# Longer runs of narrow matmuls, each begun after its copies, in one hybrid decoder layer

## The chip, the core and the metric

The kernel is one program on one core of a Trainium2 chip. Its time is the device time of one execution in microseconds (us). The profile shows one further execution, engine by engine: PE is the matrix engine (PEld its weight loads), DVE the vector engine, ACT the scalar engine, POOL the general engine, and SP the engine that issues most transfers.

## What is computed

One step of one decoder layer for two request groups: a prompt of 1024 tokens and 8 decode requests of 4 new tokens each with 1024 tokens of cache.

```python
h = rms_norm(x, g_pre);  u = h @ w_in              # q, k, v, gates of both head groups
# NSA, 8 heads on 2 k/v heads: three attentions, mixed by gates
o_n = g0 * attend(q, compressed_blocks) + g1 * attend(q, top16_blocks) + g2 * attend(q, window_512)
# FoX, 8 heads: softmax attention with accumulated forget gates in the logits
logit = (q @ k.T) * HEAD_DIM ** -0.5 + (cq[t] - ck[s])
o_f = masked_softmax(logit, k_pos <= q_pos) @ v
x = x + rms_norm(concat(o_n * silu(z_n), o_f * silu(z_f)) @ w_out, g_post)
x = x + (p @ w_pproj) * sigmoid(x @ w_pgate)
```

The decode requests compute the same, with keys and values gathered by page from caches in main memory.

## The kernel before

The work of the prompt runs in stages: input projections and compression, FoX attention over four pairs of heads (`fox(j)`, with projections of the next pair in between), NSA attention over four pairs of heads (`nsa(j, ...)`, eight tiles of 128 queries each), output projection, and the last gated addition. The decode requests' attention is written as a generator, `sample_steps()`: `sam_nsa` for two groups of four requests (`gq`), then `sam_fox` for the same two groups. `nsa` calls `advance(w)` after each piece of its own work, which takes some steps of that generator, so decode attention is spread over the NSA tiles.

Program text is not the order on the engines. The framework keeps a priority for each instruction (its place in the program, unless a block changes it), plays the program through a timeline of its own when it is built, and fixes each engine's order from that. Each engine then runs its list strictly in order, with semaphore waits. `add_manual_dep` adds an edge: a NoSync edge only orders two instructions, a Sync edge also makes the later one wait for the earlier one's end.

What the change touches, by names and lines of the kernel before:

- `evac` (L90 to L95) copies a PSUM tile to SBUF, two of three times on ACT (L93), else on DVE (L95).
- `turn` (L655) transposes blocks of probabilities `S` on PE (L659) into a PSUM tile `ps_pt`, of which there are three during NSA, and `evac` copies them back.
- `pv_pairs` (FoX, L676) and `pv_shared` (NSA, L697 and L703) multiply those by values. Their matmuls have 64 output rows, so they use half of PE's columns, and already stand in one order by `follow`.
- `score4` (L823) makes the scores of four decode requests: four matmuls with 32 output rows each, one to each quarter of PE's columns. The quarter is `32 * bl` for request `bl`.
- In `sam_fox`, keys `kp` are transposed (L1207), copied to tiles `ktf` (one of eight buffers named `kt`), and used by score matmuls (L1213) in two halves of eight per chunk of two pages; there are four chunks per group. Values `vp` are used at L1242, and the new tokens' values at L1246.
- In `sam_nsa`, `pv4` (L1129) multiplies probabilities `pts` by selected-branch values `pg` and window values `pgw`; `ktw` are the window keys, `kt_n` the new tokens' keys.

In the profile 128\*32 means a matmul with 128 contraction rows and 32 output rows; float32 matmuls that are no transposes are listed as two instructions each, so x2 is one matmul.

Of the kernel before, what the change touches and what calls it, by code (L numbers as in the profile page):

```python
# [12 lines left out]
AF = mybir.ActivationFunctionType  # L13
# [31 lines left out]
def tile_hymba_step(ctx: ExitStack, tc: tile.TileContext, I: dict, O: dict):  # L45
    nc = tc.nc
# [21 lines left out]
    def mm_tile(tag="fl"):  # L68
        return pst[1].tile([128, 512], F32, name="ps_" + tag, tag=tag, bufs=pst[2][tag])
# [122 lines left out]
    for g0 in (0, 4):  # L192
# [14 lines left out]
        for k in range(KD):  # L207
            ps = mm_tile(("fl", "sc")[k % 2])
# [446 lines left out]
    def turn(S, b0, nb):  # L655
        ps = mm_tile("pt")
        for x in range(nb):
            for a in range(2):
                nc.tensor.transpose(ps[:, (2 * x + a) * 128:(2 * x + a + 1) * 128],  # L659
                                    S[:, a, (b0 + x) * 128:(b0 + x + 1) * 128], ident)  # L660
        evac(S[:, :, b0 * 128:(b0 + nb) * 128].rearrange("p a (x c) -> p x a c", c=128),
             ps[:, :nb * 256].rearrange("p (x a c) -> p x a c", a=2, c=128))

    def follow(ins):

        for x, y in zip(ins, ins[1:]):
            tc.add_manual_dep(y.ins, x.ins.name, mybir.DependencyInfo(mybir.DependencyClass.NoSync,
                                                                      mybir.DependencyReason.DATA), reason="one stretch")

    def pv_pairs(pv, S, V, nblk, mix):  # L670
        for b0 in range(0, nblk, 2):
            turn(S, b0, min(2, nblk - b0))
        ins = []
        for b in reversed(range(nblk)):
            for a in range(2):
                ins.append(nc.tensor.matmul(pv[64 * a:64 * a + 64, :128], lhsT=V[:, b, 64 * a:64 * a + 64],  # L676
                                            rhs=S[:, a, b * 128:b * 128 + 128], start=b == nblk - 1, stop=b == 0))
        follow(ins)
        evac(mix, pv[:, :128], 0.5)

    def pv_shared(pv, S, s3, V, nblk, g, mix):


        odd = nblk % 2
        ps = mm_tile("pt")
        nc.tensor.transpose(ps[:, :128], s3, ident)
        evac(s3, ps[:, :128])
        if odd:
            turn(S, nblk - 1, 1)
            advance(1)  # L690
        for b0 in range(0, nblk - odd, 2):
            turn(S, b0, 2)
            advance(2)
        ins = []
        for b0 in reversed(range(0, nblk - odd, 2)):
            for x in range(2):
                ins.append(nc.tensor.matmul(pv[64 * x:64 * x + 64, :256], lhsT=V[b0 + x],  # L697
                                            rhs=S[:, :, (b0 + x) * 128:(b0 + x + 1) * 128],
                                            start=b0 == nblk - odd - 2, stop=False))
        for k in range(odd + 1):  # L700
            for x in range(2):
                v, p = (V[nblk - 1], S[:, x, (nblk - 1) * 128:nblk * 128]) if k < odd else (vcz[:, g, x], s3)
                ins.append(nc.tensor.matmul(pv[64 * x:64 * x + 64, 128 * x:128 * x + 128], lhsT=v, rhs=p,  # L703
                                            start=False, stop=k == odd))
        follow(ins)
# [383 lines left out]
    def sam_nsa(gq, cmp):  # L1089
# [4 lines left out]
        pgs, kts = [], []  # L1094
        for b in bs:
            pg2, kt = [], []
            for u in range(2):
# [7 lines left out]
                evac(kt[u], ps)  # L1105
# [6 lines left out]
        for c in range(2):  # L1112
            ps = mm_tile("pt")
            score4(ps, q, [[kt[c]] for kt in kts])
            nc.vector.tensor_tensor(sl[:, c * 512:(c + 1) * 512], ps, sb[:, c * 512:(c + 1) * 512], op=OP.add)
            yield
# [10 lines left out]
        def pv4(lhs, rhs, first, last):  # L1127
            for bl in range(4):
                nc.tensor.matmul(pv[32 * bl:32 * bl + 32], lhsT=lhs(bl), rhs=rhs(bl), start=first, stop=last)  # L1129
# [5 lines left out]
        pgs, kts = [], []  # L1135
        for b in bs:
# [6 lines left out]
            evac(kt, ps)  # L1143
# [5 lines left out]
        score4(ps, q, [[kt] for kt in kts])  # L1149
# [8 lines left out]
        for x in range(4):  # L1158
            pv4(lambda bl: pts[:, x, row4(bl)], lambda bl: pgs[bl][:, x, 128:256], False, False)
            yield  # L1160
        pv4(lambda bl: pts[:32, 4, row4(bl)], lambda bl: sv_n[:, 1], False, True)
# [15 lines left out]
    def sam_fox(gq):  # L1177
# [13 lines left out]
        for c in range(4):  # L1191
# [6 lines left out]
            sc = mm_tile("sv")  # L1198
            for j0 in (0, 2):
                kts = []  # L1200
                for kp in kps:
# [6 lines left out]
                    evac(kt, ps.rearrange("p (j c) -> p j c", c=256))  # L1208
                    yield
                    kts.append(kt)  # L1210
# [22 lines left out]
        for x in range(8):  # L1233
# [7 lines left out]
            for bl in range(4):  # L1241
                nc.tensor.matmul(pv[32 * bl:32 * bl + 32], lhsT=pts[:, x, 32 * bl:32 * bl + 32], rhs=vps[bl][:, x % 2],  # L1242
                                 start=x == 0, stop=False)
            yield
        for bl in range(4):
            nc.tensor.matmul(pv[32 * bl:32 * bl + 32], lhsT=pts[:32, 8, 32 * bl:32 * bl + 32], rhs=sv_f,  # L1246
                             start=False, stop=True)
# [270 lines left out]
```

## Time and profile before

| | us |
|---|---|
| median of 3 runs | 1294.2 (1292.38 to 1298.24) |
| the profiled execution, its own time | 1289.5 |
| its span, first to last instruction | 1287.7 |
| PE busy | 1194.4 (93%) |
| DVE busy | 670.0 (52%) |
| ACT busy | 604.1 (47%) |
| POOL busy | 312.8 (24%) |
| mean granted PE clock, share of full speed | 0.978 |

A busy share is the share of time in which at least one instruction of an engine was under way. Idle time of an engine that is not the bottleneck costs nothing, and a busy PE is not PE at its peak: a matmul that uses a quarter of the columns counts as busy like any other.

### The profile page before, as it was taken

What the parts mean: (1) busy time and instruction counts of PE and PEld (TensorE: products, weight loads), DVE (VectorE), ACT (ScalarE), POOL (GpSimd) and SP (SyncE); (2) the same over time, 40 slices, a digit from 0 to 9 for tenths busy, and PEclk for the clock granted to TensorE, in tenths of its full rate; (3) what the DMA queues carried; (4) which work ended last, traced back from release to release, by engine and by line L of the source; (5) the groups of instructions that cost most, each with busy time, mean ns of one, the idle gap of its engine ahead of it and who ended that gap; (6) DMA issues with size and microseconds to landing.
All of it is one profiled execution on the core that took longest, in us unless ns stands there. A gap on an engine that the chain in (4) does not pass through costs nothing. (4 is left out here: it accounts for less than half of the span.)

```text
span 1287.7 us, 23713 instructions
## 1 busy us (share of the span) xinstructions
PE 1194.4 (93%) x8106; PEld 981.2 (76%) x8106; DVE 670.0 (52%) x2062; ACT 604.1 (47%) x1415; POOL 312.8 (24%) x433
## 2 busy tenths in 40 slices
PE   3899989999999999999888899999999798999998
PEld 3798979989899898898865666564664576877776
DVE  4614455335655565553475677575455746443222
ACT  6724453244544555543465676574465742231121
POOL 2510100232222221312222232222112523131212
PEclk8999989999999999999988999999999998999999
DMA  7534311337321313224452543436645475532221
GB/s 243 137 93 136 83 48 49 96 90 227 90 55 48 106 53 95 68 76 149 136 159 95 161 132 127 153 124 223 193 138 174 140 240 171 165 139 82 71 74 38
DMA packets 142731, 157.04 MB, mean 122 GB/s; under 512 B 16586, under 2 KB 109546, under 8 KB 142418
## 3 DMA queue, kind: packets, MB, share of 16 engines
q1 hardware_dynamic: 141378, 151.06, 38.1%
q10 hardware_dynamic: 1152, 4.19, 0.9%
q8 instruction: 64, 1.05, 0.3%
q14 instruction: 57, 0.47, 0.1%
q0 software_dynamic: 80, 0.26, 0.1%
HBM read 128.30 MB, written 36.38 MB: 128 GB/s over the span
## 5 line engine op out<-in xcount | busy, mean ns | idle before, releaser
L243 PE MATMUL ps_fl<-ht,wh 128*128 128x352 f32 x1440 | 368.0, 329 | 5.6 <-DVE os L511 3.7
L243 PEld LDWEIGHTS ps_fl<-ht,wh 128*128 128x128 f32 x1440 | 256.6, 191 | 10.5 <-DVE os L511 4.0
L243 PE MATMUL ps_fl<-ht,wl 128*128 128x352 f32 x720 | 236.7, 329 | 0.0
L641 ACT ACTIVATE s<-s,m 128x64 f32<-128x64 f32 (+8 forms) x256 | 164.5, 644 | 59.6 <-DVE m L639 56.6
L83 POOL TENSOR_TENSOR wl<-wr,wh 128x256 fp32r<-128x256 f32 x120 | 89.1, 748 | 261.1 <-ACT wh L82 258.1
L644 POOL TENSOR_SCALAR s<-s,rs 128x64 f32<-128x64 f32 (+8 forms) x160 | 93.1, 601 | 234.6 <-DVE rs L1002 129.1
L243 PEld LDWEIGHTS ps_fl<-ht,wl 128*128 128x128 f32 x720 | 137.0, 190 | 1.1 <-issue 0.4
L633 PE MATMUL ps_sc<-kh,q 128*128 128x320 f32 (+12 forms) x304 | 117.3, 390 | 16.7 <-DVE m L639 10.7
L659 PE MATMUL ps_pt<-cst,s 128*128 128x128 f32 x816 | 127.0, 282 | 2.6 <-ACT s L93 1.0
L639 DVE CUSTOM_DVE_ANT_0 s<-ps_sc,bias 128x128 f32<-128x128 f32 (+10 forms) x224 | 80.4, 389 | 79.4 <-PE ps_pv L703 23.5
L659 PEld LDWEIGHTS ps_pt<-cst,s 128*128 128x128 f32 x816 | 97.1, 143 | 22.0 <-issue 5.6
L93 ACT ACTIVATE s<-ps_pt 128x512 f32<-128x512 f32 (+2 forms) x164 | 86.3, 538 | 56.3 <-PE ps_pt L659 44.6
L634 PE MATMUL ps_sc<-kl,q 128*128 128x320 f32 (+12 forms) x304 | 101.3, 336 | 1.5 <-DVE kl L622 1.5
L633 PEld LDWEIGHTS ps_sc<-kh,q 128*128 128x128 f32 x304 | 58.5, 192 | 50.5 <-DVE m L639 17.6
L639 DVE CUSTOM_DVE_ANT_0 s<-ps_sc,bias,m 128x320 f32<-128x320 f32 (+10 forms) x168 | 87.1, 523 | 7.0 <-PE ps_sc L634 3.4
L82 ACT CAST wh<-wr 128x256 fp32r<-128x256 f32 x120 | 47.7, 404 | 68.5 <-PE ps_fl L243 40.5
L95 DVE COPY s<-ps_pt 128x512 f32<-128x512 f32 (+2 forms) x84 | 49.8, 593 | 36.9 <-PE ps_pt L659 34.2
L769 POOL TENSOR_TENSOR mc<-bias,cst 128x128 f32<-128x128 f32 x64 | 30.2, 476 | 148.7 <-DVE m L639 134.7
L634 PEld LDWEIGHTS ps_sc<-kl,q 128*128 128x128 f32 x304 | 59.0, 194 | 3.7 <-DVE kl L622 1.7
L647 DVE TENSOR_SCALAR s<-s,rs 128x128 f32<-128x128 f32 (+7 forms) x96 | 54.5, 595 | 1.9
L1305 PE MATMUL ps_sc<-fwh,xh 128*128 128x512 f32 x128 | 50.8, 397 | 2.1 <-ACT xh L82 2.1
L1305 PE MATMUL ps_sc<-fwl,xh 128*128 128x512 f32 x128 | 50.1, 391 | 0.0
(444 smaller groups left out, 2191.1 us busy)
## 6 DMA issues: line engine op xcount, KB each, us to landing
kp<-in_cache_fox_kv_dram SPq DMA_DIRECT2D x64, 256.0 KB
vp<-in_cache_fox_kv_dram SPq DMA_DIRECT2D x64, 256.0 KB
wr<-in_w_in_dram SPq DMA_DIRECT2D x120, 128.0 KB
pg<-in_cache_cmp_kv_dram SPq DMA_DIRECT2D x64, 128.0 KB
pg<-in_cache_slc_kv_dram SPq DMA_DIRECT2D x64, 128.0 KB
d_g<-d_r SPq DMA_DIRECT2D x1, 4800.0 KB
bias<-d_g SPq DMA_DIRECT2D x8, 520.0 KB
X<-in_x_prompt_dram SPq DMA_DIRECT2D x8, 512.0 KB
```

Source lines behind the costliest of these rows:

```text
L83: (l_eng or nc.vector).tensor_tensor(l, src, h.bitcast(F32), op=OP.subtract)
L93: nc.scalar.activation(out, in_, AF.Copy, scale=1.0 if scale is None else scale)
L95: nc.vector.tensor_copy(out, in_)
L243: nc.tensor.matmul(ps[:, :CH], lhsT=w[k // 2][:, k % 2], rhs=HT[k][:, hl, s], start=n == 0, stop=n == 3 * KD - 1)
L633: nc.tensor.matmul(out, lhsT=qi, rhs=ks[0][:, k0:k0 + n], start=True, stop=False)
L634: nc.tensor.matmul(out, lhsT=qi, rhs=ks[1][:, k0:k0 + n], start=False, stop=True)
L639: nc.vector.tensor_tensor_reduce(o, p, bi, scale=-1.0, scalar=BIG if x == 0 else m, op0=OP.add, op1=OP.min, accum_out=m)
L641: nc.scalar.activation(s_ap, s_ap, AF.Exp, scale=-1.0, bias=m, accum_out=ssum)
L644: nc.gpsimd.tensor_scalar(s_ap, s_ap, r, 0.0, op0=OP.mult, op1=OP.add)
L647: nc.vector.tensor_scalar(s_ap, s_ap, r, None, op0=OP.mult)
L659: nc.tensor.transpose(ps[:, (2 * x + a) * 128:(2 * x + a + 1) * 128], S[:, a, (b0 + x) * 128:(b0 + x + 1) * 128], ident)
L1305: nc.tensor.matmul(o, lhsT=a[al][:, k], rhs=w[k][wl][:, c * 512:(c + 1) * 512], start=k == 0 and x == 0, stop=k == nk - 1 and x == 2)
```

## The change

A helper `stretch()` raises the priority of what is traced in it by 4000 places. Value and decode-score matmuls are put in such blocks and tied to one order by `follow`; where `follow` gets a list of copies (`after`), the first matmul of the run waits for all of them. FoX decode scores are gathered to runs of 16 (a whole chunk) in place of two times 8, the decode values of `sam_nsa` to runs of 32 and 16, and those of `sam_fox` to runs of 8. A step that now does the work of several yields their number, and `advance` counts it so.

```diff
     def evac(out, in_, scale=None):
...
-            nc.scalar.activation(out, in_, AF.Copy, scale=1.0 if scale is None else scale)
-        else:
-            nc.vector.tensor_copy(out, in_)
+            return nc.scalar.activation(out, in_, AF.Copy, scale=1.0 if scale is None else scale)
+        return nc.vector.tensor_copy(out, in_)
...
+    def stretch():
+        return tc.high_priority(offset=4000)
+
-    def follow(ins):
+    def follow(ins, after=()):
+        for x in after:
+            tc.add_manual_dep(ins[0].ins, x.ins.name, mybir.DependencyInfo(mybir.DependencyClass.Sync,
+                                                                           mybir.DependencyReason.DATA), reason="stretch")
         for x, y in zip(ins, ins[1:]):
...
     def pv_pairs(pv, S, V, nblk, mix):
+        ev = []
         for b0 in range(0, nblk, 2):
-            turn(S, b0, min(2, nblk - b0))
+            ev.append(turn(S, b0, min(2, nblk - b0)))
         ins = []
-        for b in reversed(range(nblk)):
...
+        with stretch():
+            for b in reversed(range(nblk)):
...
-        follow(ins)
+        follow(ins, ev)
...
-    def score4(ps, lhs, rhs):
+    def score4(ps, lhs, rhs, after=()):
         nx = len(rhs[0])
-        for x in range(nx):
-            for bl in range(4):
-                nc.tensor.matmul(ps[32 * bl:32 * bl + 32], lhsT=lhs[bl][x], rhs=rhs[bl][x], start=x == 0, stop=x == nx - 1)
+        with stretch():
+            follow([nc.tensor.matmul(ps[32 * bl:32 * bl + 32], lhsT=lhs[bl][x], rhs=rhs[bl][x], start=x == 0,
+                                     stop=x == nx - 1) for x in range(nx) for bl in range(4)], after)
...
         while done < (seen - 20) * 0.601:
-            done += 1
-            if next(steps, 0) is None:
-                continue
-            break
+            r = next(steps, 0)
+            if r == 0:
+                break
+            done += r or 1
...
-        for x in range(8):
-            pv4(lambda bl: pts[:, x, row4(bl)], lambda bl: pgs[bl][x // 4][:, x % 4, 128:256], x == 0, False)
-            yield
-        pv4(lambda bl: pts[:32, 8, row4(bl)], lambda bl: sv_n[:, 0], False, False)
+        pv4(range(8), lambda bl, x: pts[:, x, row4(bl)], lambda bl, x: pgs[bl][x // 4][:, x % 4, 128:256], True, False)
+        pv4((8,), lambda bl, x: pts[:32, 8, row4(bl)], lambda bl, x: sv_n[:, 0], False, False)
+        yield 8
...
-        score4(ps, q, [[kt] for kt in kts])
+        score4(ps, q, [[kt] for kt in kts], ev)
         psn = mm_tile("pt")
         score4(psn[:, :32], q, [[kt_n[:, 1]]] * 4)
...
-                for j in range(2):
-                    for bl in range(4):
-                        nc.tensor.matmul(sc[row4(bl), :256], lhsT=q[bl][j0 + j], rhs=kts[bl][:, j],
-                                         start=j0 + j == 0, stop=j0 + j == 3)
-                yield
+                    kts[bl, j0] = kt
+            with stretch():
+                follow([nc.tensor.matmul(sc[row4(bl), :256], lhsT=q[bl][j], rhs=kts[bl, j // 2 * 2][:, j % 2],
+                                         start=j == 0, stop=j == 3) for j in range(4) for bl in range(4)], ev)
+            yield 2
...
-            for bl in range(4):
-                nc.tensor.matmul(pv[32 * bl:32 * bl + 32], lhsT=pts[:, x, 32 * bl:32 * bl + 32], rhs=vps[bl][:, x % 2],
-                                 start=x == 0, stop=False)
-            yield
+            if x % 2:
+                with stretch():
+                    follow([nc.tensor.matmul(pv[row4(bl)], lhsT=pts[:, y, row4(bl)], rhs=vps[bl][:, y % 2],
+                                             start=y == 0, stop=False) for y in (x - 1, x) for bl in range(4)])
+                yield 2
```

`pv_shared` is changed as `pv_pairs` is.

How PE's order moves is seen at three places. The first is the first chunks of the FoX decode scores on PE, before: `ktf` are decode scores, `kp` transposes of decode keys, `ps_sc` scores of a prompt tile, and `cst,s` transposes of prompt probabilities.

```order
L1213 MATMUL ps_sv<-ktf,qs_f 32x256
L659 MATMUL ps_pt<-cst,s 128x128 x4
L1213 MATMUL ps_sv<-ktf,qs_f 32x256
L659 MATMUL ps_pt<-cst,s 128x128 x4
L633 MATMUL ps_sc<-kh,q_11015 128x192
L634 MATMUL ps_sc<-kl,q_11015 128x192
L633 MATMUL ps_sc<-kh,q_11015 128x128
L634 MATMUL ps_sc<-kl,q_11015 128x128
L1207 MATMUL ps_pt<-cst,kp 128x128 x4
L633 MATMUL ps_sc<-kh,q_11016 128x192
L634 MATMUL ps_sc<-kl,q_11016 128x192
L1213 MATMUL ps_sv<-ktf,qs_f 32x256 x5
```

The same engine in the change, at the second run of the second group (a run's copies are those of transposes further up).

```order
L658 MATMUL ps_pt<-cst,s 128x128 x4
L1215 MATMUL ps_pt<-cst,kp 128x128 x4
L658 MATMUL ps_pt<-cst,s 128x128 x4
L632 MATMUL ps_sc<-kh,q_13035 128x128
L633 MATMUL ps_sc<-kl,q_13035 128x128
L632 MATMUL ps_sc<-kh,q_13036 128x192
L633 MATMUL ps_sc<-kl,q_13036 128x192
L1215 MATMUL ps_pt<-cst,kp 128x128 x4
L1220 MATMUL ps_sv<-ktf,qs_f 32x256 x16
L1215 MATMUL ps_pt<-cst,kp 128x128 x4
```

Scores that stood singly between wide matmuls now stand 16 in a row.

The second place is the window scores of the second decode group on PE, before: `ktw` are four scores of 512 columns, `kt_n` four of 32 columns.

```order
L633 MATMUL ps_sc<-kh,q_9336 128x320
L634 MATMUL ps_sc<-kl,q_9336 128x320
L823 MATMUL ps_pt<-ktw,qs_n 32x512 x4
L823 MATMUL ps_pt<-kt_n,qs_n 32x32 x4
L633 MATMUL ps_sc<-kh,q_9335 128x480
L634 MATMUL ps_sc<-kl,q_9335 128x480
```

In the change:

```order
L658 MATMUL ps_pt<-cst,s 128x128 x4
L632 MATMUL ps_sc<-kh,q_9335 128x480
L633 MATMUL ps_sc<-kl,q_9335 128x480
L831 MATMUL ps_pt<-ktw,qs_n 32x512
L831 MATMUL ps_pt<-kt_n,qs_n 32x32
L831 MATMUL ps_pt<-ktw,qs_n 32x512
L831 MATMUL ps_pt<-kt_n,qs_n 32x32
```

Two more such pairs follow: the two runs, each tied within itself, now alternate. In the first group they alternate too.

The third place is the FoX decode values of the second group on PE, before (`vp` are the values, `pts` the probabilities).

```order
L1242 MATMUL ps_sv<-vp,pts 32x512
L659 MATMUL ps_pt<-cst,s 128x128 x4
L633 MATMUL ps_sc<-kh,q_13035 128x416
L634 MATMUL ps_sc<-kl,q_13035 128x416
L659 MATMUL ps_pt<-cst,s 128x128 x4
L1242 MATMUL ps_sv<-vp,pts 32x512
L633 MATMUL ps_sc<-kh,q_13035 128x416
L634 MATMUL ps_sc<-kl,q_13035 128x416
L1242 MATMUL ps_sv<-vp,pts 32x512 x4
```

In the change:

```order
L1250 MATMUL ps_sv<-vp,pts 32x512
L632 MATMUL ps_sc<-kh,q_13035 128x416
L633 MATMUL ps_sc<-kl,q_13035 128x416
L632 MATMUL ps_sc<-kh,q_13035 128x416
L633 MATMUL ps_sc<-kl,q_13035 128x416
L1250 MATMUL ps_sv<-vp,pts 32x512
L632 MATMUL ps_sc<-kh,q_13035 128x320
L633 MATMUL ps_sc<-kl,q_13035 128x320
L1250 MATMUL ps_sv<-vp,pts 32x512 x4
```

These runs get no list of copies to wait for, and stay in pieces: values of each request come by their own transfers.

## Rows read from the trace of the kernel before

**Rows 1.** The page's first part: busy us, share of the span, instructions.

```profile
PE 1194.4 (93%) x8106; PEld 981.2 (76%) x8106; DVE 670.0 (52%) x2062; ACT 604.1 (47%) x1415; POOL 312.8 (24%) x433
```

**Rows 2.** Busy time by stretch (from:to, length), granted PE clock, transfers.

```profile
690.00:795.00 105.00, 96.34 (x890) 69.45 (x887) 74.40 (x307) 70.50 (x187) 33.74 (x57) 1.00 0.45 147
795.00:895.00 100.00, 97.05 (x715) 58.55 (x714) 63.38 (x230) 62.81 (x160) 22.17 (x43) 1.00 0.49 159
895.00:995.00 100.00, 97.95 (x728) 59.40 (x726) 54.30 (x212) 53.89 (x146) 20.38 (x36) 1.00 0.53 169
995.00:1042.00 47.00, 34.85 (x242) 26.09 (x241) 33.93 (x98) 29.93 (x60) 21.95 (x19) 0.93 0.45 145
```

**Rows 3.** Costliest groups, whole span: busy us, mean ns, idle before and releasers.

```profile
L1213 PE MATMUL ps_sv<-ktf,qs_f 128*32 128x256 f32 x256 | 41.7, 389 | 0.2
L697 PE MATMUL ps_pv<-s,VW 128*64 128x256 f32 x224 | 35.1, 397 | 7.9 <-ACT s L93 4.3 <-DVE s L95 3.3 <-DVE mix L710 0.3
L1242 PE MATMUL ps_sv<-vp,pts 128*32 128x512 f32 x128 | 25.3, 600 | 0.1
```

**Rows 4.** Timeline of PE in one FoX decode chunk: start us, length us.

```profile
901.59 0.66 PE L1207 MATMUL ps_pt<-cst,kp 128*128 128x128 f32 x4
902.08 0.60 PE L659 MATMUL ps_pt<-cst,s 128*128 128x128 f32 x4
902.61 0.62 PE L1213 MATMUL ps_sv<-ktf,qs_f 128*32 128x256 f32 x2
903.16 0.66 PE L1207 MATMUL ps_pt<-cst,kp 128*128 128x128 f32 x4
903.75 1.05 PE L1213 MATMUL ps_sv<-ktf,qs_f 128*32 128x256 f32 x10
904.73 0.66 PE L659 MATMUL ps_pt<-cst,s 128*128 128x128 f32 x4
```

**Rows 5.** Timeline of PE: the first and the last of 55 pieces of these scores.

```profile
795.47 0.62 PE L1213 MATMUL ps_sv<-ktf,qs_f 128*32 128x256 f32 x2
...
961.43 1.05 PE L1213 MATMUL ps_sv<-ktf,qs_f 128*32 128x256 f32 x10
```

**Rows 6.** Timeline of PE at the FoX decode values.

```profile
970.84 3.64 PE L1242 MATMUL ps_sv<-vp,pts 128*32 128x512 f32 x32
974.41 0.42 PE L633 MATMUL ps_sc<-kh,q 128*128 128x320 f32 x1
...
976.62 1.05 PE L1242 MATMUL ps_sv<-vp,pts 128*32 128x512 f32 x2
977.60 0.41 PE L633 MATMUL ps_sc<-kh,q 128*128 128x320 f32 x1
```

**Rows 7.** Timeline of PE at the window scores, first and second group.

```profile
714.20 0.26 PE L823 MATMUL ps_pt<-kt_n,qs_n 128*32 128x32 f32 x6
714.64 0.59 PE L823 MATMUL ps_pt<-ktw,qs_n 128*32 128x512 f32 x1
715.07 0.22 PE L823 MATMUL ps_pt<-kt_n,qs_n 128*32 128x32 f32 x2
...
774.17 1.11 PE L823 MATMUL ps_pt<-ktw,qs_n 128*32 128x512 f32 x8
775.06 0.29 PE L823 MATMUL ps_pt<-kt_n,qs_n 128*32 128x32 f32 x8
775.28 0.49 PE L633 MATMUL ps_sc<-kh,q 128*128 128x480 f32 x1
```

**Rows 8.** Groups of the stretch 795 to 995: key transposes and their copies.

```profile
L1207 PE MATMUL ps_pt<-cst,kp 128*128 128x128 f32 x245 | 36.8, 279 | 1.0 <-DVE s L95 0.5 <-ACT ktf L93 0.5
...
L93 ACT ACTIVATE ktf<-ps_pt 128x512 f32<-128x512 f32 x43 | 25.0, 592 | 16.8 <-PE ps_pt L1207 16.6
...
L95 DVE COPY ktf<-ps_pt 128x512 f32<-128x512 f32 x20 | 13.8, 690 | 11.7 <-PE ps_pt L1207 11.3
```

**Rows 9.** Timeline of PE at a prompt tile's values; in brackets idle before, releaser.

```profile
998.93 0.83 PE L659 MATMUL ps_pt<-cst,s 128*128 128x128 f32 x6
1000.54 1.08 PE L697 MATMUL ps_pv<-s,VW 128*64 128x256 f32 x8 [0.78 <-ACT s L93]
```

More of the change, by code (lines that the diff above doesn't have):

```diff
@@ L670, in pv_pairs @@
     def pv_pairs(pv, S, V, nblk, mix):
+        ev = []
         for b0 in range(0, nblk, 2):
-            turn(S, b0, min(2, nblk - b0))
+            ev.append(turn(S, b0, min(2, nblk - b0)))
         ins = []
-        for b in reversed(range(nblk)):
-            for a in range(2):
-                ins.append(nc.tensor.matmul(pv[64 * a:64 * a + 64, :128], lhsT=V[:, b, 64 * a:64 * a + 64],
-                                            rhs=S[:, a, b * 128:b * 128 + 128], start=b == nblk - 1, stop=b == 0))
-        follow(ins)
+        with stretch():
+            for b in reversed(range(nblk)):
+                for a in range(2):
+                    ins.append(nc.tensor.matmul(pv[64 * a:64 * a + 64, :128], lhsT=V[:, b, 64 * a:64 * a + 64],
+                                                rhs=S[:, a, b * 128:b * 128 + 128], start=b == nblk - 1, stop=b == 0))
+        follow(ins, ev)
         evac(mix, pv[:, :128], 0.5)
@@ L686, in pv_shared @@
         nc.tensor.transpose(ps[:, :128], s3, ident)
-        evac(s3, ps[:, :128])
+        ev = [evac(s3, ps[:, :128])]
         if odd:
-            turn(S, nblk - 1, 1)
+            ev.append(turn(S, nblk - 1, 1))
             advance(1)
         for b0 in range(0, nblk - odd, 2):
-            turn(S, b0, 2)
+            ev.append(turn(S, b0, 2))
             advance(2)
         ins = []
[L695 to L705, printed above, removed]
+        with stretch():
+            for b0 in reversed(range(0, nblk - odd, 2)):
+                for x in range(2):
+                    ins.append(nc.tensor.matmul(pv[64 * x:64 * x + 64, :256], lhsT=V[b0 + x],
+                                                rhs=S[:, :, (b0 + x) * 128:(b0 + x + 1) * 128],
+                                                start=b0 == nblk - odd - 2, stop=False))
+            for k in range(odd + 1):
+                for x in range(2):
+                    v, p = (V[nblk - 1], S[:, x, (nblk - 1) * 128:nblk * 128]) if k < odd else (vcz[:, g, x], s3)
+                    ins.append(nc.tensor.matmul(pv[64 * x:64 * x + 64, 128 * x:128 * x + 128], lhsT=v, rhs=p,
+                                                start=False, stop=k == odd))
+        follow(ins, ev)
         for x in range(2):
@@ L1092, in sam_nsa @@
         q = [[qs_n[:, b]] for b in bs]
-        pgs, kts = [], []
+        pgs, kts, ev = [], [], ([], [])
         for b in bs:
@@ L1125, in sam_nsa, with pv4 @@
         pv = mm_tile("sv")[:, :128]
-        def pv4(lhs, rhs, first, last):
-            for bl in range(4):
-                nc.tensor.matmul(pv[32 * bl:32 * bl + 32], lhsT=lhs(bl), rhs=rhs(bl), start=first, stop=last)
-        for x in range(8):
-            pv4(lambda bl: pts[:, x, row4(bl)], lambda bl: pgs[bl][x // 4][:, x % 4, 128:256], x == 0, False)
-            yield
-        pv4(lambda bl: pts[:32, 8, row4(bl)], lambda bl: sv_n[:, 0], False, False)
-        pgs, kts = [], []
+        def pv4(xs, lhs, rhs, first, last):
+            with stretch():
+                follow([nc.tensor.matmul(pv[32 * bl:32 * bl + 32], lhsT=lhs(bl, x), rhs=rhs(bl, x),
+                                         start=first and x == xs[0], stop=last) for x in xs for bl in range(4)])
+        pv4(range(8), lambda bl, x: pts[:, x, row4(bl)], lambda bl, x: pgs[bl][x // 4][:, x % 4, 128:256], True, False)
+        pv4((8,), lambda bl, x: pts[:32, 8, row4(bl)], lambda bl, x: sv_n[:, 0], False, False)
+        yield 8
+        pgs, kts, ev = [], [], []
         for b in bs:
@@ L1240, in sam_fox @@
                     vps.append(vp)
-            for bl in range(4):
-                nc.tensor.matmul(pv[32 * bl:32 * bl + 32], lhsT=pts[:, x, 32 * bl:32 * bl + 32], rhs=vps[bl][:, x % 2],
-                                 start=x == 0, stop=False)
[L1244 to L1247, printed above, removed]
+            if x % 2:
+                with stretch():
+                    follow([nc.tensor.matmul(pv[row4(bl)], lhsT=pts[:, y, row4(bl)], rhs=vps[bl][:, y % 2],
+                                             start=y == 0, stop=False) for y in (x - 1, x) for bl in range(4)])
+                yield 2
+        with stretch():
+            follow([nc.tensor.matmul(pv[row4(bl)], lhsT=pts[:32, 8, row4(bl)], rhs=sv_f, start=False, stop=True)
+                    for bl in range(4)])
         om = sp.tile([128, 8, 64], F32, name="omf", tag="s_l")
```

22 lines of the change are left out of this document (11 added, 11 removed).

## Prediction

> **What bounds the kernel now.** I read the page's busy shares first: PE is under way for 1194.4 us, 93% of the span, the next engine (DVE) for 670.0 [rows 1]. That is a mean, so I cut the part that the change touches into stretches [rows 2]. From 690 to 795 us the prompt's NSA tiles share PE with NSA decode; from 795 to 995 with FoX decode; from 995 to 1042 the last NSA tiles are alone. In the 200 us of FoX decode PE is busy for 97.05 + 97.95 = 195.0 us, DVE for 117.7 and ACT for 116.7, at full clock. So PE is the bound there. Alone, the NSA tiles fill PE only to 34.85 of 47 us, 74%: there the chain of softmax and copies sets the pace.
>
> Busy does not mean well used. The groups show 41.7 us for the FoX decode scores [rows 3]: 128 matmuls of 256 columns. The timeline shows why [rows 4]. A lone score (x2) at 902.61 holds PE until the next instruction starts at 903.16, 0.55 us. Five scores (x10) at 903.75 hold it until 904.73, 0.98 us. So four more scores, one to each quarter of the columns, take 0.98 - 0.55 = 0.43 us together, and a lone one costs 0.43 us too, plus 0.12 us that each piece pays at its end. At its start a piece pays about 0.09 us: the four transposes at 902.08 last 0.60 us in all, of which the last one is 0.28 (the mean in [rows 8]), so they start (0.60 - 0.28) / 3 = 0.11 us apart; the next instruction is due 4 x 0.11 = 0.44 us on, at 902.52, and the narrow one starts at 902.61. A piece therefore costs about 0.09 + 0.12 = 0.21 us around its work. Each turn from one tile shape to another is about 0.1 us.
>
> **The Trainium skill on this.** "TensorEngine Tiling (Array Packing)", section Tiling Modes, says that a change of the tiling mode drains the engine, and a change of tile within a mode does not. The trace agrees with its 0.1 us per turn. By drains alone, 395 turns in the order before and 295 after would save about 10 us by my estimate; the rows show that the larger part is the idle three quarters beside a lone score.
>
> **The change, part by part.**
>
> *FoX decode scores.* The trace has them in 55 pieces [rows 5]: 34 of one, 4 of two, 13 of five, 2 of six, and 2 longer ones that hold small scores of the new tokens as well. A one costs [rows 4] 0.55 + 0.09 = 0.64, a two the same, a five or six 0.98 + 0.09 = 1.07: 38 x 0.64 + 15 x 1.07 = 40.4, with the two long ones (about 0.9 and 2.1) 43.4 us. The order after has 9 pieces: 7 runs of 16, at 0.21 + 4 x 0.43 = 1.93, and two of eight, at 0.21 + 2 x 0.43 = 1.07; the small scores add about 0.9. Sum 16.5, so PE gives up 43.4 - 16.5 = **27 us**.
>
> *The wait at each run.* The first score now waits for the last of eight copies, and everything on PE stands behind it. A copy takes 0.59 us on ACT, 0.69 on DVE [rows 8]. In the order, the work on PE between the last key transposes of a run and the run is, at the pitches of [rows 4], 2.0 to 4.2 us for all eight runs. That covers one copy, its queue and its semaphore, so I cost the waits at nothing. Without the cover each run would stand for 0.7 us or more.
>
> *NSA decode values.* L1129 goes from 11 pieces to 5 and the new tokens' values from 6 to 4: 8 x 0.21 = **1.7 us** less. The next decode steps get no later, since the step counts as eight.
>
> *Window scores.* Here the change loses. A narrow matmul waits for its own quarter [rows 7]: the last two small ones start at 715.07, 0.43 us after the second half of the large score on that quarter (714.64), while six on other quarters started at once. In the order after, small and large scores alternate request by request, so each large one holds the next pair back: 4 x 2 x 0.43 = 3.4 us and some 0.2 us around, in place of 775.28 - 774.17 = 1.11 us. That is 2.5 us lost per group; the first group's were already split in the trace (the rows from 714.20 belong to its second piece), so I take **+4 us**, between 0 (if the large scores overlap after all) and +5.
>
> *FoX decode values.* Sixteen of them (x32) take 3.57 us, a lone one 0.98 [rows 6]. The order leaves them in about as many pieces as before (18 in the trace, 19 in the order after), since each request's pages come by transfers of their own. **0**; the 25.3 us [rows 3] stay.
>
> *Prompt values.* FoX: the runs, and the work between last transposes and run, are unchanged (median 3.6 us of PE work). **0**. NSA: the runs were whole already; the work ahead of them shrinks a little (median 1.0 to 0.9 us by the order), because higher priority starts them sooner. They waited for copies for 7.9 us of idle [rows 3], as at 1000.54, 1.61 us after the start of six transposes [rows 9]. **+1 us**, from 0 to 3. Earlier values free the two buffers of `S` earlier, which I count as nothing.
>
> *Transfers.* Page loads move by a few places on SP's list and stay the same in number; 0.
>
> **From PE's time to the clock on the wall.** Not all 27 us come off the stretch from 795 to 995, since with less decode on PE the NSA chain shows more. Both ends come from [rows 2]: if PE stays 97.5% busy, 168 us of work take 172.3 us, a gain of 27.7. If PE's idle share grows in a straight line with the decode that is gone, between 26% (no decode) and 2.5% (41.7 + 25.3 + 36.8 = 104 us of it, [rows 3, 8]), then 77 us left give 8.5% idle, 168 / 0.915 = 183.6 us, a gain of 16.4. I take the middle, 22, because PE still has more work per tile than the chain alone needs, though with less to spare. The sum is -22 - 1.7 + 4 + 1 = -18.7 us. On the profiled execution that is 1289.5 (span 1287.7 and 1.8 around it) - 18.7 = 1270.8; that execution lies 4.7 us under the median of the runs, so for runs I say 1294.2 - 18.7 = **1275.5 us**, from -13 (1281) to -24.5 (1269.7).
>
> **Rivals.**
>
> *More comes off (15%).* PE stays full, and the alternating window scores cost nothing: -27.7 - 1.7 + 1 = -28.4, 1266 us. For it: PE's 97.5%. Against: [rows 7].
>
> *The chain takes over (14%).* With scores done faster, copies, softmax and PE's waits for them set the pace, and 13 to 20 of the 27 us come back as PE waits: -18.7 + 12 to +16, 1287 to 1292 us; in effect no change. For it: the tiles' 74% when alone [rows 2], and DVE and ACT at 55 to 63% over lists that run strictly in order. Against: PE waited for hardly anything there (5 us idle in 200). The Trainium skill, "TensorEngine Tiling (Array Packing)", section Performance Considerations, warns of just this: tiling speeds up the matmuls, not the copies out of PSUM, which may become the bottleneck. No row here shows it yet.
>
> *Each run stands for its copies (8%).* All eight `kt` buffers now fill before a run begins, and only three `ps_pt` tiles hold transposes meanwhile, for decode and prompt alike. If PE has to stand while eight copies pass one after another, 8 x 0.6 = 4.8 us at each of eight runs, that is +38: 1275.5 + 38 = 1313 us, slower. It decides from 18.7 / 8 = 2.3 us per run on (no gain), and from 3.1 us it is slower by over 0.5%. Against: the 2.0 us or more of other work in the order.
>
> **How the numbers follow.** My forecast has 63%, its own range 1269.7 to 1282. The range for 8 in 10 takes in the first rival and reaches a little into the second: 1265 to 1288. About 0.5% (6.5 us) is what a measurement can tell from no change, so faster means under 1287.7: 63 + 15 + 3 of the second = 81%; same 12%; slower 7%.
>
> **What would show it.** Right: L1213 near 14 to 16 us busy, in runs of x32 with 1.9 us to the next instruction; the stretch of FoX decode 16 to 28 us shorter; window scores with 0.87 us between large ones; L697's idle near 9 us; the FoX stages before 640 us unchanged. Wrong: idle before L1213 on ACT or DVE copies of over 1 us a run, PE's share in that stretch under 90%, or single scores as slow within a run as outside.

## The result, and the profile after

| | before | after |
|---|---|---|
| median of runs, us | 1294.2 (1292.38 to 1298.24) | 1277.3 (1273.53 to 1279.65) |
| profiled execution, its span, us | 1289.5, 1287.7 | 1273.5, 1271.8 |

The ratio of after to before is 0.9874, with a 95% interval of 0.984 to 0.9907: 1.3% faster. In what follows ratios are to the kernel before on the same chip, since medians shift by a few us between chips.

The busy shares of the page after (busy us, share of the span, instructions), against [rows 1]:

```profile
PE 1170.5 (92%) x8106; PEld 979.6 (77%) x8106; DVE 667.4 (52%) x2062; ACT 606.5 (48%) x1415; POOL 314.8 (25%) x433
```

PE gave up 1194.4 - 1170.5 = 23.9 us, and the span fell by 15.9. The stretches that answer to [rows 2] (from:to, length, busy us of each engine, granted PE clock, transfers); FoX decode now ends some 14 us sooner, so the last two are shorter or shifted, with the last NSA tiles again about 47 us long:

```profile
690.00:795.00 105.00, 93.39 (x874) 69.19 (x872) 72.66 (x303) 70.78 (x184) 31.07 (x54) 0.97 0.44 142
795.00:895.00 100.00, 93.62 (x756) 61.77 (x753) 67.69 (x248) 65.70 (x168) 25.30 (x47) 0.97 0.54 177
895.00:980.00 85.00, 81.10 (x708) 54.72 (x706) 49.18 (x201) 53.31 (x144) 20.45 (x36) 1.00 0.58 184
980.00:1027.00 47.00, 35.70 (x244) 27.39 (x244) 34.06 (x93) 29.42 (x59) 21.81 (x19) 0.89 0.46 145
```

In FoX decode PE's share went from 97.5% to (93.62 + 81.10) / 185 = 94.4%. The groups of PE that answer to [rows 3] (busy us, mean ns, idle before):

```profile
L706 PE MATMUL ps_pv<-s,VW 128*64 128x256 f32 x224 | 36.4, 408 | 7.0 <-ACT s L93 4.8 <-DVE s L94 1.8 <-DVE mix L719 0.3
L1250 PE MATMUL ps_sv<-vp,pts 128*32 128x512 f32 x128 | 25.2, 600 | 0.4 <-DMA vp<-in_cache_fox_kv_dram 0.4
L1220 PE MATMUL ps_sv<-ktf,qs_f 128*32 128x256 f32 x256 | 17.4, 414 | 0.1
```

The scores went from 41.7 us to 17.4 and wait for nothing (0.1 us idle before them). Values `vp` and prompt values are as before. A timeline of PE at one run of sixteen scores (start us, length us), and, below it, at the window scores that answer to [rows 7]:

```profile
824.50 1.93 PE L1220 MATMUL ps_sv<-ktf,qs_f 128*32 128x256 f32 x32
826.37 0.44 PE L1215 MATMUL ps_pt<-cst,kp 128*128 128x128 f32 x2
...
777.87 1.09 PE L831 MATMUL ps_pt<-ktw,qs_n 128*32 128x512 f32 x8
778.72 0.29 PE L831 MATMUL ps_pt<-kt_n,qs_n 128*32 128x32 f32 x8
778.95 0.48 PE L632 MATMUL ps_sc<-kh,q 128*128 128x480 f32 x1
```

The run holds PE for 1.87 us until the next instruction starts. The window scores still take 778.95 - 777.87 = 1.08 us: all four large ones ran together, although the list has a small one between any two. So matmuls on different quarters do not start strictly in the list's order, as was said above of every engine.

To see what became of the time, I cut each trace at the first key transposes of FoX decode (L1215) and at its last new-token values (the end of the group after L1250). These windows of before and of after are:

```profile
790.70:993.90 203.20, 198.20 (x1476) 120.26 (x1475) 118.85 (x447) 118.01 (x310) 45.79 (x83) 1.00 0.52 167
```

```profile
792.60:980.00 187.40, 177.12 (x1481) 118.14 (x1479) 118.26 (x453) 120.00 (x313) 47.06 (x83) 0.98 0.56 182
```

So FoX decode is 203.2 - 187.4 = 15.8 us shorter, which is the whole gain in span: PE is busy 21.1 us less and idle 10.3 in place of 5.0 us. (Before it, the NSA tiles with NSA decode take 2.3 us longer, counted from their first values, 150.7 against 148.4 us; after it 2.0 us less.) The waits of PE there are many and small (us in total, times, longest):

```profile
PE ps_pt L658 <- DVE s L94: 1.7, 1, 1.7
PE ps_sc L632 <- DVE m L638: 1.2, 4, 0.6
PE ps_pv L706 <- DVE mix L719: 1.2, 2, 0.7
PE ps_pv L706 <- ACT s L93: 1.2, 2, 0.9
PE ps_sc L632 <- DVE o L1261: 1.0, 1, 1.0
PE ps_sc L632 <- DVE q L962: 0.9, 1, 0.9
```

None of them is a wait of the score runs; they belong to the prompt's tiles. Behind the densest of them the clock fell, as windows of 2 us show:

```profile
804.00:806.00 2.00, 0.66 (x4) 0.42 (x4) 1.97 (x6) 1.98 (x5) 0.00 (x0) 1.00 0.60 209
806.00:808.00 2.00, 0.67 (x4) 0.42 (x5) 1.94 (x5) 1.95 (x3) 0.00 (x0) 0.73 0.71 236
808.00:810.00 2.00, 1.92 (x8) 1.64 (x8) 1.97 (x4) 1.98 (x3) 0.15 (x1) 0.50 0.58 151
810.00:812.00 2.00, 2.00 (x22) 0.85 (x24) 1.94 (x3) 1.97 (x5) 0.52 (x2) 0.50 0.94 372
812.00:814.00 2.00, 2.00 (x22) 0.73 (x15) 1.87 (x5) 0.75 (x3) 1.96 (x4) 0.56 0.08 25
```

At the start of FoX decode DVE and ACT are full (1.94 to 1.98 of 2 us), PE was busy for a third of 4 us, and was then granted 0.50, the lower level (1.2 GHz), for 6.8 us. The first run of scores, at 810.24, fell into that and took 3.57 us in place of 1.87.

### The profile page after: what moved, and what is told of

It reads as the page before. It is cut to its first block, busy times and chain, and to the rows that moved or that the text cites. A ratio compares the mean times of both kernels' runs of the same rounds, so it can differ in the third digit from the quotient of the medians.

```text
span 1271.8 us, 23735 instructions
## 1 busy us (share of the span) xinstructions
PE 1170.5 (92%) x8106; PEld 979.6 (77%) x8106; DVE 667.4 (52%) x2062; ACT 606.5 (48%) x1415; POOL 314.8 (25%) x433
## 3 DMA queue, kind: packets, MB, share of 16 engines
q8 instruction: 64, 1.05, 0.3%
## 4 chain that ended last, share of the span: by engine, by line
PE 64%; issue 9%; DMA 8%; DVE 6%; ACT 6%; POOL 3%; SPq 3%; POOLq 0%; ACTq 0%; DVEq 0%
PE ps_fl L242 20%; PE ps_sc L1313 9%; PE ps_pt L658 5%; DMA wr<-in_w_in_dram 3%; PE ps_pv L706 3%; PE ps_pv L684 3%; PE ps_sc L632 3%; PE ps_fl L1313 3%; PE ps_sc L633 2%; DVE s L638 2%; ACT s L640 2%; PE ps_sv L1250 2%; PE ps_pt L1313 2%; PE ps_pt L1215 1%; PE ps_sv L468 1%
## 5 line engine op out<-in xcount | busy, mean ns | idle before, releaser
L640 ACT ACTIVATE s<-s,m 128x640 f32<-128x640 f32 (+8 forms) x256 | 164.6, 644 | 53.6 <-DVE m L638 50.7
L638 DVE CUSTOM_DVE_ANT_0 s<-ps_sc,bias 128x128 f32<-128x128 f32 (+10 forms) x224 | 79.9, 388 | 77.9 <-PE ps_pv L712 22.5
L638 DVE CUSTOM_DVE_ANT_0 s<-ps_sc,bias,m 128x320 f32<-128x320 f32 (+10 forms) x168 | 87.1, 524 | 7.3 <-PE ps_sc L633 2.9
L778 POOL TENSOR_TENSOR mc<-bias,cst 128x128 f32<-128x128 f32 x64 | 30.2, 477 | 147.7 <-DVE m L638 133.7
```

What stands on the lines that cost most here:

```text
L638: nc.vector.tensor_tensor_reduce(o, p, bi, scale=-1.0, scalar=BIG if x == 0 else m, op0=OP.add, op1=OP.min, accum_out=m)
L640: nc.scalar.activation(s_ap, s_ap, AF.Exp, scale=-1.0, bias=m, accum_out=ssum)
```

## The experiments

**Which part does it.** e1 puts only the gathered scores into the kernel before; e2 is the kernel after with the scores as before; e3 is the kernel after in which no run waits for its list of copies; e4 the kernel after without the raised priority.

```diff
# e1: before, and in sam_fox alone
+            with stretch():
+                follow([nc.tensor.matmul(sc[row4(bl), :256], lhsT=q[bl][j], rhs=kts[bl, j // 2 * 2][:, j % 2],
+                                         start=j == 0, stop=j == 3) for j in range(4) for bl in range(4)], ev)
# e2: after, with sam_fox's scores in two halves as before (L1209 to L1215)
# e3: after, in follow
-        for x in after:
+        for x in ():
# e4: after, in stretch
-        return tc.high_priority(offset=4000)
+        return ExitStack()
```

> The kernel before with one part of the change: the FoX decode scores stand in eight runs of 16, each with its list of copies and the higher priority; all else as before. Theory (packing: the gain is PE time that lone scores wasted): the scores' busy time falls from 41.7 to about 17 us, the stretch of FoX decode from 200 to about 184 us, and the time lies 13 to 18 us under before. Rival (the gain comes from value matmuls and all the runs being taken earlier, so that buffers come free sooner): at most a third of the gain, 0 to 6 us under before.

> The changed kernel with the FoX decode scores put back as they were (two halves of eight, no list, no priority). Packing: scores busy about 42 us again, time within 4 us of before. Rival (earlier starts): 10 to 17 us under before.

> The changed kernel in which the runs keep their priority and their inner order, but get no list of copies to wait for. In PE's order the FoX decode scores then stand in 57 pieces, 38 of them single, as before. If the wait for the copies is what gathers the runs: scores busy about 42 us, time within 4 us of before. If the priority does the work: 10 us or more under before.

> The changed kernel with the lists of copies but without the higher priority. In the order the FoX decode scores stand in eight runs of 16. If the wait gathers the runs: scores busy about 17 us, time within 4 us of the changed kernel, 13 to 20 us under before. If the priority matters: PE starts runs later, buffers come free later, and the time lies 5 us or more above the changed kernel.

| | median us | ratio (95%) | scores, busy us |
|---|---|---|---|
| e1 scores only | 1274.83 | 0.9841 (0.9812 to 0.9869) | 16.9 |
| e2 all but scores | 1295.54 | 1.0008 (0.9985 to 1.003) | 42.2 |
| e3 no wait | 1297.45 | 1.0009 (0.9984 to 1.0034) | 41.7 |
| e4 no priority | 1278.62 | 0.9855 (0.9824 to 0.9886) | 16.4 |

The gathered scores are the whole gain; the rest of the change is worth nothing that can be measured. (e1 gained 20.8 us, more than the 13 to 18 expected; its FoX decode, at 188.3 us, is no shorter than that of the kernel after, so the surplus does not come from there.) And it is the list of copies that gathers them: without the priority (e4) the runs stand and cost 16.4 us, without the list they do not. In e3, with the order edges and the priority but no list, the group is as costly as before:

```profile
L1220 PE MATMUL ps_sv<-ktf,qs_f 128*32 128x256 f32 x256 | 41.7, 389 | 0.8 <-DVE sm L1224 0.8
```

The planner then places each score as soon as its own copy is there, and other work between them. The list makes the first one late, and the rest follow it at once.

The rest of the change moves waits, though. In the stretch of NSA decode (641 to 796 us), some of PE's waits in e2 and then in e1:

```profile
PE ps_pt L694 <- POOL s L643: 6.9, 5, 4.4
PE ps_pt L1080 <- POOL s_s L643: 4.3, 1, 4.3
PE ps_pt L1112 <- DVE kt L94: 2.3, 1, 2.3
```

```profile
PE ps_sc L632 <- DVE m L638: 6.0, 7, 3.3
PE ps_pv L703 <- DVE s L94: 2.5, 1, 2.5
PE ps_pt L692 <- POOL s L643: 1.4, 1, 1.4
PE ps_pt L1077 <- POOL s_s L643: 1.2, 2, 1.0
```

With it, PE stands for 6.9 us ahead of transposes of the prompt's probabilities, for their normalisation on POOL (1.4 us without it), once for 4.3 us ahead of those of the decode probabilities (1.2 without it), and once for 2.3 us for a key copy. Other waits shrink: those for `m` (L638) from 6.0 to 4.4 us, that for `s` on DVE from 2.5 to 0.9. The sum does not show on the clock. From the first values of NSA, where every kernel here has 4281 matmul instructions behind it, to the first key transposes of FoX decode, e2 took 148.4 us, before 148.4 and e1 147.7. Nor would a few us be a finding there: e2, the kernel after and e5, e6, e8, e11 and e12 have one and the same order of PE in that stretch, and took between 148.4 (e2) and 154.6 us (e8), whose ends are these rows, e2 first:

```profile
647.36 0.39 PE L712 MATMUL ps_pv<-s,vcz 128*64 128x128 f32 x4
795.72 0.60 PE L1215 MATMUL ps_pt<-cst,kp 128*128 128x128 f32 x4
```

```profile
645.98 0.39 PE L712 MATMUL ps_pv<-s,vcz 128*64 128x128 f32 x4
800.60 0.60 PE L1215 MATMUL ps_pt<-cst,kp 128*128 128x128 f32 x4
```

The kernel after has the same three waits (6.0, 3.8 and 2.4 us), and a granted clock of 0.55 at 718 to 720 us and 0.54 at 730 to 732, on either side of the one of 3.8 us.

**Does the order within a run matter?** e5 writes the sixteen scores request by request, so four in a row go to one quarter of the columns.

```diff
-                                         start=j == 0, stop=j == 3) for j in range(4) for bl in range(4)], ev)
+                                         start=j == 0, stop=j == 3) for bl in range(4) for j in range(4)], ev)
```

> The kernel after, with the sixteen FoX decode scores of a run written request by request (four in a row on one quarter of the columns) in place of head by head (four in a row on four quarters). Theory that a quarter has its own queue, so that a matmul that waits for its quarter holds back none behind it on other quarters: the run still takes about 1.9 us to the next instruction, L1220 about 17 us busy, 1277 us, within 0.5% of the kernel after. Rival, that TensorE starts matmuls strictly in the list's order: four in a row on one quarter run one after the other and the next request's wait behind them, so of 16 scores hardly any overlap: 16 x 0.43 = 6.9 us a run, L1220 about 55 us busy, about +40 us of PE, and 1300 to 1317 us. Which it is also says whether the alternating window scores (+4 us in the prediction) could cost anything at all.

e5 took 1302.44 us, a ratio of 1.0059 (1.0034 to 1.0083): slower than before. The kernel after, run beside it (e8, below), took 1280.22. The group of its scores:

```profile
L1220 PE MATMUL ps_sv<-ktf,qs_f 128*32 128x256 f32 x256 | 38.8, 388 | 0.1
```

One of its runs in the timeline of PE, and what starts next:

```profile
829.17 4.59 PE L1220 MATMUL ps_sv<-ktf,qs_f 128*32 128x256 f32 x32
833.70 0.55 PE L1215 MATMUL ps_pt<-cst,kp 128*128 128x128 f32 x3
```

A run holds PE for 833.70 - 829.17 = 4.53 us: not the 1.9 of quarters that never hold each other back, nor the 6.9 of strict order. The records of its 32 instructions (two to a score) show what lies between. A record does not name its request, but the starts fall into series 0.216 us apart. The first request's eight start at 829.172, .412, .628, .843, 830.059, .275, .491 and .707; the second request's first starts at 830.065, 6 ns behind the fifth of the first request, while three of that one still wait. The third request's first (830.958) stands 5 ns behind the fifth of the second (830.953) in the same way. All eight runs begin so, and six of them hold PE for 4.41 to 4.53 us; the first began at half clock, and the fifth stands in two pieces. So in these runs a quarter holds one instruction under way and three that wait; a fourth that would have to wait holds up everything behind it in the list. The weight loads show the same step (the first request's sixth at 830.061, the second's first at 830.063), so whether matmuls or their weight loads fill up is not told apart. Three stages of four instructions and one of eight, (12 + 8) x 0.216 = 4.3 us and the piece's 0.21, give the 4.53. The window scores put only two large and two small instructions on a quarter, which just fits, and they lost nothing. Both rivals on the order of starts were thus wrong: e5's time lies in the range of strict order (1300 to 1317 us), but with 38.8 us of scores and not its 55.

e5 is also a test of what PE time is worth. It has the order of the kernel after, with 38.8 - 17.4 = 21.4 us more of scores. Its FoX decode as a window:

```profile
795.40:1003.50 208.10, 198.22 (x1481) 129.44 (x1478) 118.62 (x453) 119.98 (x313) 47.14 (x83) 0.99 0.50 164
```

PE's longest waits in it:

```profile
PE ps_pt L658 <- DVE s L94: 1.7, 1, 1.7
PE ps_sc L632 <- DVE m L638: 1.6, 5, 0.6
PE ps_pv L706 <- DVE mix L719: 1.2, 2, 0.7
PE ps_sc L632 <- DVE o L1261: 1.0, 1, 1.0
PE ps_sc L632 <- DVE q L962: 0.9, 1, 0.9
```

PE is as busy as in the kernel before (198.22 against 198.20 us) and yet idle for 9.9 us, with nearly the waits of the kernel after. From there to the kernel after PE gives up 21.1 us, and the stretch 208.1 - 187.4 = 20.7. So PE time counts one for one, and the 5 us or so of idle come with the new order, not with PE having less to do.

**Does gathering pay for the values too, and does a smaller gathering cost less?** e6 makes each run of eight FoX decode values wait for its eight page loads; e7 is e1 with the same; e8 is the kernel after once more, on the chip of e5 to e7. e9 cuts the runs of sixteen scores into eights with four copies each. e10 is e6 with ten page buffers in place of eight and one buffer of decode score rows in place of two; both numbers stand at every use of these buffers, in NSA decode too. e11 and e12 are e6 and e9 again; the rows of the runs of eight are those of e12.

```diff
# e6, e7: load_pages returns its transfers, and in sam_fox
+                    got += load_pages([vp[:, u] for u in range(2)], b * 8 + x,
...
-                                             start=y == 0, stop=False) for y in (x - 1, x) for bl in range(4)])
+                                             start=y == 0, stop=False) for y in (x - 1, x) for bl in range(4)], got)
# e9: within the loop over j0
+                    follow([nc.tensor.matmul(sc[row4(bl), :256], lhsT=q[bl][j], rhs=kts[bl, j0][:, j % 2],
+                                             start=j == 0, stop=j == 3) for j in (j0, j0 + 1) for bl in range(4)], ev[-4:])
# e10: e6, and
-                    vp = sp.tile([128, 2, 512], F32, name="vp", tag="pg", bufs=8)
+                    vp = sp.tile([128, 2, 512], F32, name="vp", tag="pg", bufs=10)
-        s = sp.tile([128, 1056], F32, name="s_s", tag="s_s", bufs=2)
+        s = sp.tile([128, 1056], F32, name="s_s", tag="s_s", bufs=1)
```

> The kernel after, in which each run of eight FoX decode values also waits for all eight of its page loads, as the scores do for their copies. In the order 19 pieces of values become 6 (four of eight, two of sixteen). By the rows of the kernel after, a lone value holds PE for 0.98 us and sixteen take 3.57, so eight take about 1.9: 4 x 2.0 + 2 x 3.7 = 15 us in place of 25.2, 10 us less PE. Theory (gathering a run by a wait takes PE time off, and some 0.7 of it shows on the clock as it did for the scores, 16 of 22): vp about 15 us busy, 1268 to 1273 us, ratio to the kernel after 0.993 to 0.997. Rival 1: the loads come late, PE stands at the run, idle before the vp runs of 1 us or more each, no gain or a loss of up to 10 us (1277 to 1287). Rival 2: the stretch is now set by the chain of copies and softmax, the 10 us turn up as PE waits for copies: vp 15 us busy but 1275 to 1279 us.

> The kernel before with two changes alone: FoX decode scores in runs of 16 that wait for their copies, and FoX decode values in runs of 8 that wait for their page loads; window scores, NSA decode and prompt values stay in the order before. If the rest of the change is neutral (two runs gave 1.0008 and 1.0009 for what lacks the scores or their wait), this equals the run with values waiting in the kernel after, within 0.3%: 1266 to 1273 us if the values' PE time shows on the clock as the scores' did, 1273 to 1278 if the chain now sets the pace. If the extras of the change cost a little (the stretch of NSA decode grew by 2 to 3 us in the kernel after), it is 2 to 4 us below that run.

> The kernel after, unaltered, beside the other three on one chip: 1277 us, ratio 0.987 to before. It is there so that the others are read against it; the scores alone gave 0.9841 (0.9812 to 0.9869) and the whole change 0.9874 (0.984 to 0.9907) on different chips. If the extras cost nothing, it comes out at 0.984 to 0.988; if they take 3 to 4 us back, at 0.987 or above while the two packed parts alone lie lower.

> The kernel after, with each run of sixteen FoX decode scores cut in two runs of eight, each of which waits for its own four copies. PE: eight pieces more at 0.21 us is 1.7 us, so L1220 goes from 16.4 to about 18 us busy. What it tells apart is where the other idle of PE in FoX decode comes from, 5.0 us before and 9.8 to 10.6 in every kernel whose scores wait for copies. Theory, the waits come with the gathering (eight copies at once on DVE and ACT, and a run that stands for the last): half the copies to a run lower it to 6 to 8 us and the kernel is as fast or 1 to 3 us faster, 1275 to 1280 us. Rival, that idle shows because PE has less decode work to fill the tiles with: it stays at 10 us and the kernel is 1 to 2 us slower, 1279 to 1282 us.

> The kernel with gathered values, with ten page buffers in place of eight and one buffer for the decode scores' rows in place of two (there is no room for both). In that kernel PE stood 5.9 us for page loads ahead of the second and third run of values, since the loads of those pages start only when the first run has freed its buffers. Theory: two buffers more let 2 of the 8 requests' loads in question start early, and the wait falls by a part, to 3 to 5 us, 1273 to 1275 us. Rival: the last load decides, which still waits for a buffer, and runs are put earlier in the list by the planner: the wait stays at 5 to 7 us, 1275 us; or the single row buffer makes decode softmax wait and it is 1 to 3 us slower.

> The kernel with gathered values, unaltered, on the chip of the other two: 1274.8 us and a ratio of 0.9841 to before if its 5.4 us under the kernel after on its chip (1280.2) are its own; by the stretch of FoX decode alone they should be 4 us (182.4 against 186.3). If 0.987 or above, its gain over the kernel after is not to be told from none.

> The runs of eight scores once more, unaltered, since the profiled execution of the first time had its clock at half speed over long stretches (0.747 on average) and its waits can't be read beside the others. Wanted is PE's idle in FoX decode: 6 to 8 us if the waits come with the gathering of eight copies, 10 us if they come from PE having less decode work; and L1220 about 18 us busy in either case. The time, by the first run, is 0.986 of before.

| | median us | ratio (95%) | FoX decode: length, PE busy, idle, us |
|---|---|---|---|
| e6 values wait | 1274.83 | 0.9841 (0.9801 to 0.988) | 182.4, 166.1, 16.3 |
| e7 both, rest as before | 1276.45 | 0.9853 (0.9818 to 0.9889) | 184.5, 168.8, 15.7 |
| e8 after again | 1280.22 | 0.9879 (0.9851 to 0.9907) | 186.3, 175.7, 10.6 |
| e9 runs of eight | 1274.52 | 0.9857 (0.9833 to 0.988) | |
| e10 values, room | 1268.86 | 0.9809 (0.9786 to 0.9833) | 182.2, 166.5, 15.7 |
| e11 as e6 | 1272.82 | 0.9847 (0.9823 to 0.9871) | 182.5, 166.0, 16.5 |
| e12 as e9 | 1273.98 | 0.9855 (0.9809 to 0.9902) | 184.2, 175.2, 9.0 |

*Values.* In e6 the group fell as worked out, but PE now stands for loads:

```profile
L1253 PE MATMUL ps_sv<-vp,pts 128*32 128x512 f32 x128 | 15.0, 596 | 6.0 <-DMA vp<-in_cache_fox_kv_dram 5.9
```

Ten us come off PE and six come back as a wait, the one that the first rival of e6 named, so FoX decode is 3.9 us shorter than in e8. The total agrees in both runs of it (0.9841 and 0.9847, against 0.9874 and 0.9879 of the kernel after), but the intervals overlap: likely a gain of 0.3%, not shown. e7, which gathers scores and values and leaves out the rest of the change, comes to 0.9853, within the 0.3% of e6 that was expected if the rest is neutral.

*Runs of eight.* The scores take 17.1 us in e12, and idle in FoX decode is 9.0 us, between the 6 to 8 and the 10 that were expected. Halving the gathering gives back no more than 1.6 of the 5 us, so the wait for eight copies at once makes a small part of them at most. The rival, that PE has less decode work to fill the tiles with, is excluded by e5. Which moved instruction makes which wait was not traced; that stays open. In time runs of eight cannot be told from runs of sixteen (0.9857 and 0.9855 against 0.9874 and 0.9879).

*Room.* e10 beats both kernels, by 4 us against e11 on the same chip, but not by the wait for loads, which is still there (6.3 us in e11):

```profile
PE ps_sv L1253 <- DMA vp<-in_cache_fox_kv_dram: 5.1, 3, 2.9
```

FoX decode is as long as in e11. What differs is the stretch before it, here in e10 and then in e11:

```profile
641.00:786.90 145.90, 126.21 (x1084) 92.43 (x1081) 107.23 (x441) 97.38 (x260) 44.77 (x77) 0.95 0.45 140
```

```profile
641.00:795.50 154.50, 130.08 (x1105) 96.76 (x1104) 106.67 (x448) 98.64 (x265) 44.64 (x77) 0.94 0.41 126
```

PE's waits in e11 from 641 to 796 us, two of them:

```profile
PE ps_pt L1083 <- POOL s_s L646: 5.1, 1, 5.1
PE ps_pt L1115 <- DVE kt L94: 2.2, 1, 2.2
```

These two waits, which the kernel after also has, are not in e10. But the 8.6 us between the two windows are not all its doing, since e10 was ahead when they begin. The first values of NSA, in e10 and then in e11:

```profile
641.20 0.39 PE L715 MATMUL ps_pv<-s,vcz 128*64 128x128 f32 x4
```

```profile
644.52 0.39 PE L715 MATMUL ps_pv<-s,vcz 128*64 128x128 f32 x4
```

3.3 us were gained in the stages before, which neither edit touches. From there on the stretch is 145.7 against 151.0 us, 5.3 shorter, and 3.1 are given back behind FoX decode (294.4 against 291.3). It is 2.7 us under the fastest of the seven executions with the other order (148.4 to 154.6 us), so the cause is likely the new order there, but one trace does not show how much it is worth, nor which of the two edits moved the waits.

## Why the prediction was right, and which steps were not

The forecast of 1275.5 us stands 1.8 us from the 1277.3 measured. Its main step held, scores that give up PE time. The nearness of the total is in part luck: by spans FoX decode gave 6.2 us less than forecast, and against that the +1 for prompt values did not come, and 2.0 us behind FoX decode and 0.4 ahead of NSA fell off that the sum did not have. Such differences come without a change: the part behind FoX decode took 291.8 us here and 293.3 in e8, the same kernel.

- **FoX decode scores, -27 us of PE: right in mechanism, a little too large.** The busy time of the group fell by 41.7 - 17.4 = 24.3, or 41.7 - 16.4 = 25.3 in e8. The sum by pieces had put 43.4 us on the order before, 1.7 more than the row, since it put 0.64 and 1.07 us on pieces that the row counts at 0.62 and 1.05, and took the small scores in the two long ones along. In the profiled execution one run at half clock took 1.7 us more. Runs of 1.87 and 1.00 us, without the 0.09 at the start of a piece, answer to the 1.93 and 1.07 worked out with it.
- **The wait at each run, 0: right.** 0.1 us of idle ahead of L1220 in all. The rival "each run stands for its copies" falls.
- **From PE's time to the clock, -22 between -16.4 and -27.7: this step failed.** FoX decode lost 15.8 us, just outside the lower end. The straight line assumed that PE's idle share grows because decode fills less of it. e5 shows otherwise: full PE, 9.9 us of idle. What happened is a change one for one, less about 5 us of small waits that the new order brings, and less what the half clock behind them took (6.8 us at 0.50 are 3.4 us of full clock, half of it in the run at 810.24 and so within the 24.3 already). The sum is -24.3 + 3.2 + 5.3 = -15.8: the scores, the busy time that other groups gained (24.3 - 21.1, part of it by that clock), and the idle.
- **Window scores, +4: wrong.** They take 1.08 us a group, against 1.11 and a first one in two pieces before. [rows 7] showed that a matmul waits for its own quarter; that it holds back the next quarter's did not follow. It does so only from a fourth waiting instruction on (e5).
- **NSA decode values, -1.7: right on PE.** The group `pg` fell from 4.9 to 4.1 us, that of the new tokens from 2.5 to 1.7; `pgw` went from 3.2 to 3.1 only, since its run of 32 at 730.14 fell into a stretch at half clock, and is 2.3 in e2.
- **FoX decode values, 0: right** (25.3 and 25.2). **Prompt values, +1: nothing**; the idle ahead of them is 7.0 us, 0.9 less.
- **Not in the prediction:** the longer waits in NSA decode for POOL and for a key copy, and the shorter ones beside them. That stretch came out 2.3 us longer, which is the sum's 4 - 1.7 by chance: the window scores cost nothing, and the same order took from 148.4 to 154.6 us there.

"More comes off" fell by the new waits, though its part on window scores was right. "The chain takes over" was right in its sign, but of the 13 to 20 us that it would have taken only about 5 came. Its own sum does not come out: the forecast already left out 5 of the 27 us, so 13 to 20 lost are +8 to +15, 1283.5 to 1290.5 us, in place of the +12 to +16 written.

Of the signs that it named, runs of 1.87 us and unchanged stages before 640 us came. The scores' 17.4 us (14 to 16 were named), the 15.8 us of FoX decode (16 to 28), L697's idle of 7.0 us (near 9) and the window scores, whose large ones start 0.01 to 0.02 us apart and not 0.87, did not.

## What to carry to other kernels

A narrow matmul that stands alone costs the array as much as four on four quarters (0.43 us in these rows), so look at how many stand together in the order, not at the busy share; if a planner places each as soon as it can, a wait for the last operand on the first of the run is what gathers them. Write the run so that consecutive instructions go to different quarters: the same sixteen in the other order took 4.53 us in place of 1.87 and made the kernel slower than before. Before turning PE time into clock time, ask whether the new order moves other instructions next to the copies they need: here that cost about 5 us of the 21, and in e6 six of the ten us that the values gave up came back as a wait for loads. And before a few us in one trace are read as a gain, count a stretch from the same instruction in both, and see how much executions of one order differ there: 6 us in NSA decode, 1.1 in FoX decode (187.4 and 186.3).

## What the hardware showed that I had not expected

- A column quarter took instructions ahead of their turn: one under way and three waiting (e5), with the list held up from the next one on.
- Three to four us in which PE was busy for a third (804 to 808 us: 0.66 and 0.67 of 2.00) were followed by 6.8 us at a granted 0.50, so a short stall cost some 3 us more than itself. In the kernel before PE was busy for 5.69 of 8 us from 804 to 812, and the clock stayed at 1.00.
